# Attention mask products in float32r instead of bfloat16, in a hybrid decoder trunk

## The chip, the cores and the metric

One NeuronCore of a Trainium2 chip runs the whole program in one launch. The metric is device time in microseconds (us), lower is better. Engines are named as in the profile: PE is TensorE's matrix product, PEld its weight load, DVE is VectorE, ACT is ScalarE, POOL is GpSimd, SP is SyncE, which here only issues DMAs.

## The reference

Two layers, 512 tokens of width 1024 in float32. Each layer is SwiGLU (width 2816), a mixer, SwiGLU, with a residual and a layer norm behind each. The mixer joins two kinds of softmax-like attention with a gated delta rule and projects the result:

```
def diff_attention_block(q_blk, start, k1, k2, v, lam):
    causal = s[None, :] <= t[:, None]
    def probs(qi, ki):
        sc = einsum('bhqd,bhkd->bhqk', qi, ki) * A_QK_DIM ** -0.5
        return softmax(where(causal, sc, -inf), axis=-1)
    w = probs(q1, k1) - lam * probs(q2, k2)
    return einsum('bhqk,bhkd->bhqd', w, v)            # 4 heads, 2 x 32 wide, values 64

def stick_breaking_block(q_blk, start, k, v):         # 4 heads of 64
    strict = s[None, :] < t[:, None]
    z = einsum('bhqd,bhkd->bhqk', q_blk, k) * B_HEAD_DIM ** -0.5
    log_stay = where(strict, log_sigmoid(-z), 0.0)
    log_tail = cumsum(log_stay, axis=3, reverse=True) - log_stay
    w = where(strict, exp(log_sigmoid(z) + log_tail), 0.0)
    return einsum('bhqk,bhkd->bhqd', w, v)

# the delta rule solves, in chunks, (I + strict_lower(k_beta k^T * decay)) [u, w] = rhs
# and then scans over the chunks with a state per head
```

## The kernel before

Activations stand feature-major, 128 features by 512 tokens in a tile. Every float32 matrix is split into a high and a low part in float32r, and a product of two is three PE products (`mm3`, lines 103 to 105): high x high, high x low, low x high. Weights come in chunks of 512 KB by DMA (`wraw`, line 81, mostly issued by SP), are cast by ACT (line 89, `whi`) and subtracted by DVE or POOL (line 90, `wlo`).

In the mixer, a layer's attention runs in units: a block of 128 queries (`qt`) of one head against the `n = (qt + 1) * 128` keys up to it. `scores` (line 872) makes a unit's scores in a PSUM bank: one or two products of float32r operands (line 880, one for the diff attention, two for the stick-breaking one), and then the mask product of line 881, which adds the mask to the 128 columns on the diagonal, as identity times mask. The mask is 0 or `NEG`; for it two bfloat16 constants, `identb` and `maskb`, were made at the start. Behind the mask come the row maximum on DVE (line 917), the exponential on ACT (line 467, in the helper `act`), the difference of the two softmaxes on DVE (lines 922 to 926), transposes on PE (line 904), a copy on ACT (906) and the product with the values (line 909). A unit's transposes are recorded behind the next unit's scores (`later`).

`attend(which, j)` goes through eight units of two heads. The stick-breaking attention (`which` 1) comes first in a mixer, then the projections of the delta rule, then `triangles()`: for each of four heads, products (line 594), the decays (lines 663 to 665), the matrix `LT` (line 673), its way to a scratch in DRAM (line 675), and then `base`, which reads the diagonal blocks of 16 x 16 (line 692, tile `blk`), inverts them on DVE in thirty small steps (lines 700 and 702), writes them back (lines 703 and 705) and reads the whole matrices `XT` and `X` (lines 708 and 710, the latter in a tile named `inv`). `attend(0, 0)`, the first two heads of the diff attention, is written behind `triangles()`, and in its middle the second projection of its queries and keys, whose weight products (lines 103 to 105) and stacking copies (`stack`: DVE cast of line 511, small DMAs of line 524 on SP) fill in. `delta()` doubles and joins the inverse (lines 718, 723, 738, 745); `outputs()` is the scan.

The order on each engine is not the order of the text: a scheduler takes each engine's next instruction from those that are ready by its own estimate, so an instruction more or less in one place can lay the order out anew behind it. Each engine's queue, SP's included, is then strictly in order.

The constants are loaded by POOL's DMAs in `constants()`, recorded behind the first SwiGLU's gate products. Two of the three scratch tensors are filled with zeros there, by DMAs from a small tile `zero` of the constants' pool that POOL clears at the program's start. Tiles named `lt` come from a pool of five buffers that the layer norms, the SwiGLU and the mixers share.

Of the kernel before, what the change touches and what calls it, by code (L numbers as in the profile page):

```python
# [9 lines left out]
F32 = mybir.dt.float32  # L10
F32R = mybir.dt.float32r
BF16 = mybir.dt.bfloat16
# [4 lines left out]
P = 128  # L17
# [353 lines left out]
        run((), g.pending)  # L371


NEG = -1.0e30
HEADS = 4
NC = T // P
SB = 16
# [3 lines left out]
def const_masks():  # L381
    r = np.arange(P)
    row, col = r[:, None], r[None, :]
    ms = [
        np.where(col >= row, 0.0, NEG),
        (row <= col).astype(np.float64),
    ]
    ms.append(((row // (2 * SB) == col // (2 * SB)) & (row // SB % 2 == 0) & (col // SB % 2 == 1)).astype(np.float64))
    ms.append(np.where(col <= row, 0.0, NEG))
    ms.append(np.where(col < row, 0.0, NEG))  # L390
    return np.stack(ms, axis=1).astype(np.float32)
# [31 lines left out]
def ch(c):  # L423
    return slice(c * P, (c + 1) * P)


def mixer(g, l):
    nc = g.nc
# [16 lines left out]
    def py():  # L445
        return psc.tile([P, T], F32, name="psc")
# [103 lines left out]
    n = 2 * HEADS  # L550
# [323 lines left out]
    def scores(q, k, qt, i, which):  # L874

        n = (qt + 1) * P
        dgn = ch(qt)
        sc = py()
        for j, t in enumerate(k[i]):
            nc.tensor.matmul(out=sc[:, 0:n], lhsT=q[i][0][:, dgn], rhs=t[:, 0:n], start=j == 0, stop=False)  # L880
        nc.tensor.matmul(out=sc[:, dgn], lhsT=g.identb, rhs=g.maskb[:, which], start=False, stop=True)
        return sc

    def attend(which, j, between=None):
# [13 lines left out]
    def unit(which, qt, h, po, su, col):  # L898
# [13 lines left out]
        def diff():  # L912
            mx = sm.tile([P, 2], F32, name="mx")
            pr = []
            for i in range(2):
                sc = scores(qa, ka, qt, 2 * h + i, 0)
                nc.vector.tensor_reduce(out=mx[:, i:i + 1], in_=sc[:, 0:n], axis=mybir.AxisListType.X, op=ALU.max, negate=True)
                p = at.tile([P, T], F32, name="at")
                act(out=p[:, 0:n], in_=sc[:, 0:n], func=AF.Exp, bias=mx[:, i:i + 1], accum_out=su[:, i:i + 1])
                pr.append(p)  # L920
            cf = sm.tile([P, 2], F32, name="cf")
            nc.vector.reciprocal(out=cf[:, 0:1], in_=su[:, 1:2])
            nc.vector.scalar_tensor_tensor(out=cf[:, 1:2], in0=su[:, 0:1], scalar=g.nlam[:, l:l + 1], in1=cf[:, 0:1],
                                           op0=ALU.mult, op1=ALU.mult)
            p1, p2 = pr
            nc.vector.scalar_tensor_tensor(out=p1[:, 0:n], in0=p2[:, 0:n], scalar=cf[:, 1:2], in1=p1[:, 0:n],
                                           op0=ALU.mult, op1=ALU.add)
            return lambda: values(p1)
# [150 lines left out]
def program(ctx, tc, a, out, mixer=None):  # L1079
    g = Ctx()  # L1080
    g.tc = tc
    g.nc = nc = tc.nc
    g.out = out
    g.a = a
    cp = ctx.enter_context(tc.tile_pool(name="const", bufs=1))
    g.cp = cp
    g.dp = ctx.enter_context(tc.tile_pool(name="scratch", bufs=1, space=bass.MemoryType.DRAM))
    g.wr = ctx.enter_context(tc.tile_pool(name="wr", bufs=2))
    g.ws = ctx.enter_context(tc.tile_pool(name="ws", bufs=WS))
    g.xp = ctx.enter_context(tc.tile_pool(name="xp", bufs=24))  # L1090
    g.lnp = ctx.enter_context(tc.tile_pool(name="lnp", bufs=5))
    g.sm = ctx.enter_context(tc.tile_pool(name="sm", bufs=2))
    g.ps = ctx.enter_context(tc.tile_pool(name="ps", bufs=2, space=bass.MemoryType.PSUM, reuse_waits="tile"))
    g.st = Stream(g, a["w"])

    g.ones = cp.tile([P, P], F32, name="ones")
    nc.gpsimd.memset(g.ones, 1.0)
    g.ident = cp.tile([P, P], F32, name="ident")
    nc.gpsimd.affine_select(out=g.ident, in_=g.ones, pattern=[[-1, P]], compare_op=ALU.is_equal, fill=0.0,
                            base=0, channel_multiplier=1)  # L1100

    def after(later, first, sync=False):
        kind = mybir.DependencyClass.Sync if sync else mybir.DependencyClass.NoSync
        tc.add_manual_dep(later.ins, first.ins.name, mybir.DependencyInfo(kind, mybir.DependencyReason.DATA), reason="order")

    g.after = after
    nln = DEPTH * 3 * KD
    g.lng = cp.tile([P, nln], F32, name="lng")
    g.lnb = cp.tile([P, nln], F32, name="lnb")
    small = ("conv", "dtb", "alog", "dng", "dfg", "sbg")  # L1110
    for nm in small:
        setattr(g, nm, cp.tile(list(a[nm].shape), F32, name=nm))
    g.mask = cp.tile([P, NMASK - 2, P], F32, name="mask")
    g.maskb = cp.tile([P, 2, P], BF16, name="maskb")
    g.identb = cp.tile([P, P], BF16, name="identb")
    nc.vector.tensor_copy(out=g.identb, in_=g.ident)
    g.ba = cp.tile([P, DEPTH, KD, 4 * HEADS], F32R, name="ba")
    g.nlam = cp.tile([P, DEPTH], F32, name="nlam")
    n = HEADS * NC * SLAB // P
    zero = cp.tile([P, n // 16], F32, name="zero")  # L1120
    nc.gpsimd.memset(zero, 0.0)
    g.scr = [g.dp.tile([P, n], F32, name=f"scr{i}") for i in range(3)]

    def constants():

        def load(out, in_):
            g.after(nc.gpsimd.dma_start(out=out, in_=in_), g.mark, True)

        raw = g.lnp.tile(list(a["ba"].shape), F32, name="lt")
        load(raw, a["ba"])  # L1130
        part = g.ba[:, :, :, 0:2 * HEADS]
        nc.scalar.copy(out=part, in_=raw)
        nc.vector.tensor_tensor(out=g.ba[:, :, :, 2 * HEADS:], in0=raw, in1=part.bitcast(F32), op=ALU.subtract)
        load(g.lng, a["lng"])
        load(g.lnb, a["lnb"])
        load(g.mask, a["mask"][:, 0:NMASK - 2])
        for nm in small:
            load(getattr(g, nm), a[nm])
        lb = g.lnp.tile([P, DEPTH, 4, 32], F32, name="lt")
        load(lb, a["lamb"])  # L1140
        mb = g.lnp.tile([P, 2, P], F32, name="lt")
        load(mb, a["mask"][:, NMASK - 2:NMASK])
        nc.vector.tensor_copy(out=g.maskb, in_=mb)
        for l in range(DEPTH):
            init = 0.8 - 0.6 * math.exp(-0.3 * l)
            nc.vector.tensor_scalar(out=g.dfg[:, l:l + 1], in0=g.dfg[:, l:l + 1], scalar1=1.0 - init, scalar2=None, op0=ALU.mult)
            dv = lb[:, l].rearrange("p (a b) d -> p a b d", b=2)
            nc.vector.tensor_tensor(out=dv[:, :, 0], in0=dv[:, :, 0], in1=dv[:, :, 1], op=ALU.mult)
            le = g.sm.tile([P, 2], F32, name="lam")
            nc.vector.tensor_reduce(out=le, in_=dv[:, :, 0], axis=mybir.AxisListType.X, op=ALU.add)  # L1150
            nc.scalar.activation(out=le, in_=le, func=AF.Exp)
            lv = g.nlam[:, l:l + 1]
            nc.vector.tensor_tensor(out=lv, in0=le[:, 1:2], in1=le[:, 0:1], op=ALU.subtract)
            nc.vector.tensor_scalar(out=lv, in0=lv, scalar1=-init, scalar2=None, op0=ALU.add)
        for t in g.scr[1:]:
            load(t.rearrange("p (a b) -> p a b", a=16), zero.unsqueeze(1).to_broadcast([P, 16, n // 16]))

    g.constants = constants
    g.wctx = ExitStack()

    def more_weights():
        g.wx = g.wctx.enter_context(tc.tile_pool(name="wx", bufs=WX, side="right", reuse_waits="tile"))

    g.more_weights = more_weights
    more_weights()
    g.x = []
    g.st.use([g.ws])
    with tc.tile_pool(name="x0", bufs=KD) as x0:
        for k in range(KD):
            if k % 4 == 0:  # L1170
                for b in range(2):
                    g.st.get(2 * k + b * PC)
            t = x0.tile([P, T], F32, name="x0")
            nc.sync.dma_start(out=t, in_=a["xT"][k * P:(k + 1) * P])
            hi = g.xp.tile([P, T], F32R, name="x")
            lo = g.xp.tile([P, T], F32R, name="x")
            nc.scalar.copy(out=hi, in_=t)  # L1177
            nc.vector.tensor_tensor(out=lo, in0=t, in1=hi.bitcast(F32), op=ALU.subtract)
            g.x.append((hi, lo))
    g.pending = ()  # L1180
    for l in range(DEPTH):
        ffn(g, 3 * l, False, True)
        if mixer:
            mixer(g, l)
        ffn(g, 3 * l + 2, l == DEPTH - 1, False)
    g.wctx.close()
# [72 lines left out]
```

## Time and profile before

| | |
|---|---|
| time, median of 3 runs | 2249.18 us (2244.98 to 2249.8) |
| the profiled execution | 2250.16 us, span 2248.4 us |
| PE busy | 2138.2 us, 95% of the span |
| PE's weight load busy | 1782.6 us, 79% |
| DVE, ACT, POOL busy | 1169.6, 907.9, 377.5 us |
| granted clock of TensorE | 0.985 of full speed, mean of the span |

Busy times of PE are unions of intervals that overlap: a product's row lasts until its last result is written, while the next has begun. The share of the span therefore says little on how much faster a product could come behind the one before it; the distance from one start to the next does. Where the clock is granted at 0.5, TensorE runs at 1.2 GHz, else at 2.4 GHz; a share between them is a mean over the stretch.

### The profile page before, as it was taken

To read this page: it belongs to the slowest core of one execution; us is meant where nothing else is said; L and a number is where in the kernel's file an instruction comes from. 1 tells how busy PE (TensorE), PEld (TensorE's weight loads), DVE (VectorE), ACT (ScalarE), POOL (GpSimd) and SP (SyncE) were. 2 spreads that over 40 slices of the span, in tenths; PEclk is the share of its full clock that TensorE was granted. 3 is DMA by queue.
4 is the path that set the end of the run, shared out by engine and by line. 5 is a ranking of instruction groups with operands and counts; after the bars stand their busy time and mean duration, and the time that the engine had idled before them with its cause. 6 is when DMAs were issued, how large, how long until landed. Compare 5 with 4: busy or idle time off the path is not lost. (4 is left out here: it accounts for less than half of the span.)

```text
span 2248.4 us, 30132 instructions
## 1 busy us (share of the span) xinstructions
PE 2138.2 (95%) x11382; PEld 1782.6 (79%) x11382; DVE 1169.6 (52%) x2363; ACT 907.9 (40%) x1801; POOL 377.5 (17%) x327
## 2 busy tenths in 40 slices
PE   8999999999798999999999999999987989999997
PEld 7888889777677888888888888897776768888886
DVE  4533436386578833343663334263774788333426
ACT  4333324575464533332443333245753535333313
POOL 1100011426204400000130000023461234000010
PEclk9999999999899999999999999999998999999998
DMA  6423323514512233332333333234144123333322
GB/s 190 125 94 95 98 75 104 139 40 122 129 58 72 84 109 94 94 94 75 116 109 95 94 94 94 66 104 131 57 133 109 48 85 94 95 96 100 95 66 94
DMA packets 90898, 217.32 MB, mean 97 GB/s; under 512 B 21968, under 2 KB 36336, under 8 KB 90752
## 3 DMA queue, kind: packets, MB, share of 16 engines
q1 hardware_dynamic: 82848, 187.47, 27.5%
q10 hardware_dynamic: 6912, 25.17, 3.8%
q0 software_dynamic: 992, 2.75, 0.7%
q8 instruction: 90, 1.47, 0.3%
q14 instruction: 56, 0.46, 0.1%
HBM read 193.83 MB, written 6.83 MB: 89 GB/s over the span
## 5 line engine op out<-in xcount | busy, mean ns | idle before, releaser
L89 ACT CAST whi<-wraw 128x512 fp32r<-128x512 f32 x692 | 421.4, 619 | 959.4 <-PE pd L104 755.1
L90 DVE TENSOR_TENSOR wlo<-wraw,whi 128x512 fp32r<-128x512 f32 x580 | 431.0, 751 | 658.6 <-ACT whi L89 647.4
L103 PE MATMUL pd<-x,whi 128*128 128x512 f32 (+1 forms) x1920 | 726.7, 380 | 12.9 <-ACT x L1177 6.2
L105 PE MATMUL pd<-x,wlo 128*128 128x512 f32 (+1 forms) x1920 | 728.3, 380 | 3.2 <-DVE wlo L90 3.2
L104 PE MATMUL pd<-x,whi 128*128 128x512 f32 (+1 forms) x1920 | 727.7, 379 | 1.6 <-POOL x L231 1.3
L103 PEld LDWEIGHTS pd<-x,whi 128*128 128x128 f32 x1920 | 365.8, 191 | 77.5 <-ACT x L1177 6.2
L105 PEld LDWEIGHTS pd<-x,wlo 128*128 128x128 f32 x1920 | 366.2, 191 | 67.4 <-DVE wlo L90 3.4
L104 PEld LDWEIGHTS pd<-x,whi 128*128 128x128 f32 x1920 | 366.2, 191 | 66.8 <-POOL x L231 3.0
L103 PE MATMUL pd<-hhi,whi 128*128 128x512 f32 (+1 forms) x880 | 307.7, 350 | 0.0
L104 PE MATMUL pd<-hlo,whi 128*128 128x512 f32 (+1 forms) x880 | 307.7, 350 | 0.0
L105 PE MATMUL pd<-hhi,wlo 128*128 128x512 f32 (+1 forms) x880 | 307.3, 349 | 0.0
L168 POOL TENSOR_TENSOR lt<-lt 128x512 f32<-128x512 f32 x26 | 38.9, 1497 | 1065.3 <-ACT lt L165 1065.3
L103 PEld LDWEIGHTS pd<-hhi,whi 128*128 128x128 f32 x880 | 165.5, 188 | 24.4
L105 PEld LDWEIGHTS pd<-hhi,wlo 128*128 128x128 f32 x880 | 165.4, 188 | 24.1
L104 PEld LDWEIGHTS pd<-hlo,whi 128*128 128x128 f32 x880 | 165.5, 188 | 24.1
L90 POOL TENSOR_TENSOR wlo<-wraw,whi 128x512 fp32r<-128x512 f32 x112 | 150.2, 1357 | 138.7 <-ACT whi L89 70.1
L259 DVE TENSOR_TENSOR lt<-pd,lt 128x512 f32<-128x512 f32 x88 | 60.4, 689 | 111.9 <-PE pd L105 110.7
L231 POOL TENSOR_TENSOR x<-x 128x256 fp32r<-128x256 f32 x60 | 45.1, 753 | 162.5 <-ACT x L229 132.7
L134 POOL TENSOR_TENSOR x<-x 128x512 f32<-128x512 f32 x48 | 70.9, 1522 | 0.0
L261 DVE TENSOR_TENSOR hlo<-lt,hhi 128x512 fp32r<-128x512 f32 x88 | 67.0, 765 | 6.3
L165 ACT ACTIVATE lt<-x 128x256 f32<-128x256 f32 (+1 forms) x58 | 29.7, 512 | 95.8 <-DVE x L163 95.5
L568 DVE SCALAR_TENSOR_TENSOR kqv<-pd,conv,kqv 128x511 f32<-128x511 f32 (+2 forms) x72 | 53.5, 743 | 20.1 <-ACT kqv L566 18.9
(309 smaller groups left out, 2287.9 us busy)
## 6 DMA issues: line engine op xcount, KB each, us to landing
wraw<-in_w SPq DMA_DIRECT2D x308, 512.0 KB, 3.5
wraw<-in_w ACTq DMA_DIRECT2D x48, 512.0 KB, 3.6
kqv<-kqv SPq DMA_DIRECT2D x128, 64.0 KB, 2.0
kqv<-kqv SPq DMA_DIRECT2D x48, 128.0 KB, 4.7
scr<-zero POOLq DMA_DIRECT2D x2, 1032.0 KB, 11.1
x<-in_xT SPq DMA_DIRECT2D x8, 256.0 KB, 5.5
scr<-inv SPq DMA_DIRECT2D x8, 256.0 KB, 2.7
XT<-scr SPq DMA_DIRECT2D x8, 256.0 KB, 4.8
```

The source lines that it names most:

```text
L89: nc.scalar.copy(out=hi, in_=r)
L90: (eng or self.eng or nc.vector).tensor_tensor(out=lo, in0=r, in1=hi.bitcast(F32), op=ALU.subtract)
L103: nc.tensor.matmul(out=out, lhsT=whi, rhs=xhi, start=first, stop=False)
L104: nc.tensor.matmul(out=out, lhsT=whi, rhs=xlo, start=False, stop=False)
L105: nc.tensor.matmul(out=out, lhsT=wlo, rhs=xhi, start=False, stop=last)
L134: i = g.nc.gpsimd.tensor_tensor(out=t, in0=xhi.bitcast(F32), in1=xlo.bitcast(F32), op=ALU.add)
L165: nc.scalar.activation(out=sq[:, r], in_=t[:, r], func=AF.Square)
L168: eng.tensor_tensor(out=self.acc2[:, r], in0=self.acc2[:, r], in1=sq[:, r], op=ALU.add)
L231: eng.tensor_tensor(out=xlo[:, r], in0=t[:, r], in1=xhi[:, r].bitcast(F32), op=ALU.subtract)
L259: nc.vector.tensor_tensor(out=sg, in0=pu, in1=sg, op=ALU.mult)
L261: nc.vector.tensor_tensor(out=hlo, in0=sg, in1=hhi.bitcast(F32), op=ALU.subtract)
L568: nc.vector.scalar_tensor_tensor(out=y[:, s:], in0=p[:, :T - s], scalar=wc[:, 3 - s:4 - s], in1=y[:, s:], op0=ALU.mult, op1=ALU.add)
```

## The change

The identity and the mask of the mask products become float32r tiles (`identr`, `maskr`), as the scores' operands are; `NEG` becomes a power of two. Where a bfloat16 product has a weight-load instruction of its own in the program, a float32r product loads its weights itself, so 96 load instructions leave the program (48 mask products in each layer). The constants' pool gives up the tile `zero`; the zeros come from an `lt` buffer instead, cleared and sent to the scratch behind the other loads of `constants()`.

```
-NEG = -1.0e30
+NEG = -2.0 ** 100
...
-        nc.tensor.matmul(out=sc[:, dgn], lhsT=g.identb, rhs=g.maskb[:, which], start=False, stop=True)
+        nc.tensor.matmul(out=sc[:, dgn], lhsT=g.identr, rhs=g.maskr[:, which], start=False, stop=True)
...
-    g.maskb = cp.tile([P, 2, P], BF16, name="maskb")
-    g.identb = cp.tile([P, P], BF16, name="identb")
-    nc.vector.tensor_copy(out=g.identb, in_=g.ident)
+    g.maskr = cp.tile([P, 2, P], F32R, name="maskr")
+    g.identr = cp.tile([P, P], F32R, name="identr")
+    nc.vector.tensor_copy(out=g.identr, in_=g.ident)
...
-    zero = cp.tile([P, n // 16], F32, name="zero")
-    nc.gpsimd.memset(zero, 0.0)
...
-        nc.vector.tensor_copy(out=g.maskb, in_=mb)
+        nc.vector.tensor_copy(out=g.maskr, in_=mb)
...
+        zero = g.lnp.tile([P, n // 16], F32, name="lt")
+        nc.gpsimd.memset(zero, 0.0)
         for t in g.scr[1:]:
             load(t.rearrange("p (a b) -> p a b", a=16), zero.unsqueeze(1).to_broadcast([P, 16, n // 16]))
```

The order changes with it. On PE, in the first layer's `attend(0, 0)`, the units with 512 keys stand in a row before (`psc` is the scores' bank, `pd` a bank of weight products, `pt` one of transposes):

```order
L880 MATMUL psc<-kqv 128x512
L881 LDWEIGHTS identb
L881 MATMUL psc<-maskb,identb 128x128
L880 MATMUL psc<-kqv 128x512
L881 LDWEIGHTS identb
L881 MATMUL psc<-maskb,identb 128x128
L904 MATMUL pt<-ident,at 128x128 x3
L880 MATMUL psc<-kqv 128x512
```

In the new program the same place of PE's order reads:

```order
L880 MATMUL psc<-kqv 128x512
L881 MATMUL psc<-maskr,identr 128x128
L104 MATMUL pd<-x,whi 128x512
L105 MATMUL pd<-x,wlo 128x512
L103 MATMUL pd<-x,whi 128x512
L104 MATMUL pd<-x,whi 128x512
L105 MATMUL pd<-x,wlo 128x512
L103 MATMUL pd<-x,whi 128x512
L104 MATMUL pd<-x,whi 128x512
L105 MATMUL pd<-x,wlo 128x512
L904 MATMUL pt<-ident,at 128x128 x3
```

Eight weight products have moved between the first score of 512 columns and the transposes. A little later on PE, in the units with 256 keys of the same two heads, the order of before has weight products between the attention's (`po` is the bank of the output):

```order
L880 MATMUL psc<-kqv 128x256
L881 LDWEIGHTS identb
L881 MATMUL psc<-maskb,identb 128x128
L103 MATMUL pd<-x,whi 128x512
L104 MATMUL pd<-x,whi 128x512
L909 MATMUL po<-kqv,at 128x64 x4
L904 MATMUL pt<-ident,at 128x128 x4
L105 MATMUL pd<-x,wlo 128x512
L880 MATMUL psc<-kqv 128x128
```

and now the units with 256 and 128 keys follow each other:

```order
L880 MATMUL psc<-kqv 128x256
L881 MATMUL psc<-maskr,identr 128x128
L909 MATMUL po<-kqv,at 128x64 x4
L904 MATMUL pt<-ident,at 128x128 x4
L880 MATMUL psc<-kqv 128x128
```

The weight products are gone from there. On SP, around the inverse of the first layer, the four scratch writes, the weight load, the read of the blocks and the small copies of the stacked queries and keys stand so before:

```order
L675 DMA scr_98<-inv 128x4x128 x4
L81 DMA wraw<-in_w 128x1024
L692 DMA blk<-scr_98 128x16x16
L524 DMA kqv<-kqv 32x512 x12
L703 DMA scr_99<-blk 128x16x16
```

and so in the new program (the scratch tensors' numbers have moved by two):

```order
L675 DMA scr_96<-inv 128x4x128 x3
L524 DMA kqv<-kqv 32x512 x2
L675 DMA scr_96<-inv 128x4x128
L524 DMA kqv<-kqv 32x512 x2
L81 DMA wraw<-in_w 128x1024
L692 DMA blk<-scr_96 128x16x16
L81 DMA wraw<-in_w 128x1024
L524 DMA kqv<-kqv 32x512 x7
L703 DMA scr_97<-blk 128x16x16
```

Four of the small copies now stand ahead of the read of the blocks, two of them ahead of the last scratch write.

## Rows read from the trace of the kernel before

**Rows 1.** The page, part 1: engine, busy us (share), instructions.

```profile
PE 2138.2 (95%) x11382; PEld 1782.6 (79%) x11382; DVE 1169.6 (52%) x2363; ACT 907.9 (40%) x1801; POOL 377.5 (17%) x327
```

**Rows 2.** Line 881 alone (duration ns min/median/max); then costliest groups (busy us, mean ns).

```profile
L881 PEld LDWEIGHTS <-identb x96: 94/96/153, 432.6 to 1772.2; 128*128 128x128 bf16 x96
L881 PE MATMUL psc<-maskb,identb x96: 219/230/330, 432.6 to 1772.3; 128*128 128x128 bf16 x96
...
L103 PEld LDWEIGHTS pd<-x,whi 128*128 128x128 f32 x1920 | 365.8, 191 | 77.5 <-ACT x L1177 6.2
```

**Rows 3.** Windows: stretch us, length, busy us (instructions) by engine, granted clock, DMA share, GB/s.

```profile
565.00:581.00 16.00, 12.20 (x52) 8.80 (x50) 13.18 (x36) 9.54 (x27) 9.32 (x9) 0.69 0.55 132
581.00:595.00 14.00, 11.11 (x77) 9.30 (x76) 12.41 (x54) 7.14 (x23) 2.55 (x2) 0.99 0.17 40
...
1680.00:1695.00 15.00, 10.85 (x47) 7.89 (x46) 12.60 (x34) 8.66 (x25) 8.42 (x9) 0.77 0.57 140
```

**Rows 4.** Timeline of PE, 568 to 603 us: start, us, ..., [idle before <-releaser].

```profile
569.90 0.45 PE L880 MATMUL psc<-kqv 128*128 128x384 f32 x1 [1.54 <-ACT at L467]
...
572.31 0.80 PE L880 MATMUL psc<-kqv 128*128 128x512 f32 x1 [1.27 <-ACT at L467]
...
601.92 2.04 PE L718 MATMUL pa<-inv,lt 128*128 128x128 f32 x8 [3.36 <-DMA inv<-scr]
```

**Rows 5.** Timeline of PE, around a mask before weight products.

```profile
446.20 0.39 PE L105 MATMUL pd<-x,wlo 128*128 128x512 f32 x1
446.43 0.40 PE L880 MATMUL psc<-kqv 128*128 128x256 f32 x2
446.68 0.23 PE L881 MATMUL psc<-maskb,identb 128*128 128x128 bf16 x1
446.71 0.47 PE L103 MATMUL pd<-x,whi 128*128 128x512 f32 x1
447.03 0.40 PE L104 MATMUL pd<-x,whi 128*128 128x512 f32 x1
```

**Rows 6.** Timeline of PE, a mask before transposes.

```profile
439.51 0.23 PE L881 MATMUL psc<-maskb,identb 128*128 128x128 bf16 x1
439.58 0.50 PE L904 MATMUL pt<-ident,at 128*128 128x128 f32 x3
```

**Rows 7.** Timeline of PE, other products of 128 columns.

```profile
545.81 1.06 PE L594 MATMUL po<-kqv 128*128 128x128 f32 x8
546.71 1.06 PE L594 MATMUL pt<-kqv 128*128 128x128 f32 x8
...
585.71 0.22 PE L880 MATMUL psc<-kqv 128*128 128x128 f32 x1
585.78 0.23 PE L881 MATMUL psc<-maskb,identb 128*128 128x128 bf16 x1
```

**Rows 8.** Timeline of POOL, 40 to 300 us.

```profile
40.57 1.18 POOL L1127 DMA_DIRECT2D scr<-zero  x1
53.26 1.13 POOL L1127 DMA_DIRECT2D scr<-zero  x1 [11.51 <-issue]
...
234.43 0.54 POOL L1127 DMA_DIRECT2D lt<-in_mask  x1 [10.33 <-DVE hlo L261]
287.02 1.55 POOL L168 TENSOR_TENSOR lt<-lt 128x512 f32<-128x512 f32 x1 [52.05 <-ACT lt L165]
```

**Rows 9.** Timeline of DVE, 577 to 594 us.

```profile
577.66 0.16 DVE L700 TENSOR_TENSOR blkt<-blk 128x15 f32<-128x15 f32 x1
...
580.96 0.42 DVE L917 TENSOR_REDUCE mx<-psc 128x1 f32<-128x256 f32 x1 [2.39 <-PE psc L881]
...
586.04 0.29 DVE L917 TENSOR_REDUCE mx<-psc 128x1 f32<-128x128 f32 x1 [0.64 <-PE psc L881]
...
593.86 0.37 DVE L704 COPY blk<-blk 128x256 f32<-128x256 f32 x1
```

## The prediction

> **What bounds the kernel now.** I read the summary first, then the line of the changed product, then the stretch in which TensorE loses time. TensorE (PE) is busy 2138.2 of 2248.4 us, VectorE (DVE) 1169.6 us [rows 1]; so a change pays by what it takes off PE's stream, or off the moments in which PE stands still or runs slowly. The mask product is one of 96 PE instructions with a mean near 230 ns, and its own weight load takes 96 ns, against 191 ns for a load of float32r weights [rows 2]. These durations overlap from one instruction to the next, so I price everything by the distance from one start to the next.
>
> PE's losses lie thick in one place, in each of the two layers: the first two heads of the diff attention, beside the triangular inverse. From 565 to 581 us PE is busy 12.20 of 16 us at a granted clock of 0.69 (of 1.0, so 1.2 GHz for 10 of the 16 us and 2.4 GHz for the rest), and the second layer has the same at 1680 to 1695 us (0.77) [rows 3]. There PE waits 1.54 and 1.27 us for the exponentials on ScalarE (ACT), and later 3.36 us for the inverse to come back from memory [rows 4].
>
> **Price of the products themselves, before.** A 512-column weight product takes 0.23 us from start to start (446.20 to 446.43). Mask product plus the weight product behind it take 0.35 us (446.68 to 447.03). So the bf16 mask costs 0.12 us, although its row is followed 0.03 us later by the next start: the product behind it pays [rows 5]. In front of a transpose it costs 0.07 us (439.51 to 439.58) [rows 6]. In the program's order of before, 62 of the 96 masks stand before a weight or score product and 34 before something else: 62 x 0.12 + 34 x 0.07 = 9.8 us.
>
> **After.** The trace has no 128-column mask in float32r. Its nearest kin is the 128-column score product, float32r too: 0.07 us to the next start (585.71 to 585.78), but with the short bf16 load behind it, so this is the low end. With full-length loads behind them, 128-column products run at 0.11 us (eight in 0.90 us, 545.81 to 546.71). The high end is that a narrow float32r product takes as long as a 512-column one, 0.23 us [rows 5, 7]. I take 0.11 us, because in the new kernel the load behind is always a full-length one: 96 x 0.11 = 10.6 us, so **+0.8 us**, with ends at 96 x 0.07 = 6.7 us (-3.1 us) and 96 x 0.23 = 22.1 us (+12.3 us). The separate weight-load instruction of the mask goes, but the load stays.
>
> The loads in the rows differ by a factor of two, 96 against 191 ns [rows 2]. If the 95 ns more were open at each mask, 96 x 95 ns = 9.1 us would be added; it is the third rival below. What I hold against it is [rows 5]: behind the short load and its product, the next product is 0.09 us late (0.32 us to its successor instead of 0.23), so the short load's advantage is not seen in the distances. The Trainium skill has the rule that speaks against the change: by "TensorE: Matmul & The Clock Gate", section "Weight-path perf modes", a fast load reads weights 32 bits at a time, two of bf16, with no win for fp32. The factor of two in the trace agrees with it; by that rule alone the sum would be those 9.1 us higher.
>
> **What else is removed or moved.** The zeros of the scratch: their memset and two DMAs leave the place before the residual sums and stand behind the load of the mask on GpSimd (POOL). POOL issued them at about 41 and 53 us, waiting 11.51 us between the two; now it can do so from about 235 us, and is free near 250 us. The next thing that POOL does is at 287.02 us [rows 8], so some 37 us cover it: price nothing. The zeros now hold one of the five `lt` buffers until the second DMA lands, but the statistics that need that buffer back belong to the same 287 us. If the cover were gone, the stall would be of the size of that wait, 11.5 us. The early stretch gains nothing, since nothing in front of PE waited for POOL there. The casts of identity and mask on DVE stay one for one. NEG is a value.
>
> **The new order.** With 96 load instructions fewer and other operands, the scheduler lays PE's order out anew in both mixers. I counted weight products (rows of lines 103 to 105) between attention products in the first diff attention beside the inverse. From the first 512-column score to the first 256-column score: 5 before, 18 after (and 4 more just ahead). From there to the last transpose: 19 before, 2 after. Between that and the wait for the inverse: 8 before, 6 after. So PE's filling moves to where it stood still, and leaves the stretch behind. What this is worth goes by DVE, which makes the inverse (577.66 to 593.86 us, thirty small steps among the softmax) and is busy 12.41 of 14 us there [rows 3, 9]. In that time DVE itself waited for PE's scores 2.39 and 0.64 us [rows 9], while PE was at the lower clock and had weight products between the scores. Those two waits, 3.0 us, are what can go per layer; I take half, since the softmax steps in front of the inverse come a step earlier in DVE's queue and a cast stands before the last triangle: **-1.5 us per layer, -3.0 us in both**. The low end is nothing at all. The high end is both waits in full and the waits of PE for ACT (2.8 us) once, 5.8 us per layer.
>
> Against that, SyncE (SP) gets four small copies of the stacked heads around the last scratch write, and a weight load before the read of the blocks stays. SP's order is strict, so a copy that waits for DVE's cast holds the inverse back. I price that under the rivals.
>
> **The sum.** +0.8 - 3.0 = -2.2 us on the profiled execution's 2250.16 us (span 2248.4 us): 2248.0 us. The median shown, 2249.18 us, lies 1.0 us below the profiled time, so the forecast on the median is about **2247 us**.
>
> **Rivals.**
> 1. *The new order gives much more.* PE stays at 2.4 GHz through the 512-column units and DVE's waits go in full: 2 x 5.8 = 11.6 us less, +0.8: about 2238 us. For it: 10 us at 1.2 GHz per layer in [rows 3]. Against it: the filling is taken from the next stretch, where DVE, not PE, sets the pace, and the slow clock may simply come there.
> 2. *The inverse starts later (slower).* SP's four copies wait for DVE's cast of the keys, and the last scratch write and the read of the blocks wait behind them; PE has only 6 weight products (1.4 us) to cover what comes on top of its 3.36 us wait for the inverse [rows 4]. Each copy held up for a us is a us at the end. With 2 to 3 us of delay per layer and 0.5 us less cover (two products), 5 to 7 us: about 2255 us. It decides as soon as the delay passes DVE's saving of 1.5 us.
> 3. *The mask product is dear in float32r*, by its load (+9.1 us) or because a narrow product is as slow as a wide one (+12.3 us), with the order's -3.0 us: 2255 to 2258 us. Against it: the 0.07 us of the narrow score.
> 4. *Nothing happens*: the order's parts cancel and 0.11 is 0.10: 2249 us.
>
> **How the numbers follow.** Forecast (2244 to 2250 us) 0.45, rival 1 0.20, rival 2 0.16, rival 3 0.08, rival 4 0.11. A measurement of this kernel tells about 0.2%, 4.5 us, from no change: 2244.7 to 2253.7 us counts as the same. Of the forecast 0.32 lies inside and 0.13 below; of rival 2, 0.02 inside. Faster 0.20 + 0.13 = 0.33; same 0.32 + 0.11 + 0.02 = 0.45; slower 0.14 + 0.08 = 0.22. The range goes from 2237 us (rival 1 but for its end) to 2258 us (rivals 2 and 3 but for the dearest).
>
> **What would show it.** Right: from a mask product in float32r to the next start some 0.11 us, and the product behind it no longer late, 0.23 us to its successor. In the inverse's first stretch PE's waits for ACT under 1 us and the clock near 1.0, with a lower clock or new waits in the 256- and 128-column units behind; the inverse's last step no later than in before. Wrong: 0.2 us from mask to next start in float32r (rival 3); scratch writes or the read of the blocks that stand behind the small copies on SP, and a wait for the inverse well above 3.4 us (rival 2); POOL's first sum of squares after 287 us (the zeros).

## The result: 0.7% slower, and the profile after

The changed kernel takes 2264.55 us (median of 6 runs, 2258.5 to 2269.06) against 2249.46 us (2244.98 to 2251.1) of the kernel before on the same chip: ratio 1.0069, 95% interval [1.0055, 1.0084]. On another chip it came to 1.0074 [1.0059, 1.009]. The forecast was 2247 us; the time lies above the range, and above every rival in it. The profiled execution has a span of 2266.9 us at a mean granted clock of 0.979, where before had 2248.4 us and 0.985.

The first part of the page of the changed kernel, and the line of the mask products alone (weight load, product), answer [rows 1] and the first lines of [rows 2]:

```profile
PE 2148.1 (95%) x11382; PEld 1801.9 (79%) x11382; DVE 1176.8 (52%) x2363; ACT 910.0 (40%) x1801; POOL 378.8 (17%) x327
```

```profile
L881 PEld LDWEIGHTS psc<-maskr,identr x96: 186/189/333, 440.3 to 1782.9; 128*128 128x128 f32 x96
L881 PE MATMUL psc<-maskr,identr x96: 218/223/415, 440.4 to 1782.9; 128*128 128x128 f32 x96
```

PE is busy 9.9 us more and idle 8.6 us more. The load of a mask's weights doubled (96 to 189 ns), the product itself is as long as it was.

**The stretch the forecast looked at.** The windows around the first two heads of the diff attention answer [rows 3], and PE's two longest waits there answer [rows 4]:

```profile
574.00:590.00 16.00, 13.41 (x71) 10.16 (x69) 15.41 (x37) 9.02 (x26) 10.74 (x10) 0.99 0.58 146
590.00:604.00 14.00, 13.07 (x58) 11.82 (x57) 11.11 (x55) 7.62 (x25) 1.27 (x1) 0.50 0.27 72
```

```profile
587.85 0.50 PE L880 MATMUL psc<-kqv 128*128 128x512 f32 x1 [1.83 <-ACT at L467]
...
611.11 2.05 PE L718 MATMUL pa<-inv,lt 128*128 128x128 f32 x8 [4.04 <-DMA inv<-scr]
```

The first window went from a clock of 0.69 to 0.99 and PE from 12.20 to 13.41 us busy; the low clock came in the next window instead (0.99 to 0.50), and the wait for the inverse grew from 3.36 to 4.04 us (in the second layer it fell, from 4.80 to 4.18 us). From the first product of line 594 to the last of line 758, the inverse and what lies around it, the layers took 105.7 and 106.6 us before and take 103.0 and 101.3 us now (starts of those products). Three weight products, 0.7 us, have left this stretch (137 before, 134 now); the rest of the 2.7 and 5.3 us is a gain. The first product on the finished inverse (line 718) comes 1.2 and 1.4 us sooner behind the first of line 594, near the 1.5 us that were forecast.

**What is paid back ahead of it.** From a layer's first score (line 880) to the first product of line 594, the stick-breaking attention and the projections, it is 116.3 and 115.7 us before and 119.2 and 119.0 us after, with 336 weight products in each. It is so in every trace with the new order: 117.8 to 121.0 us, against 114.2 to 117.6 us in every trace with the old one. So about 3 us per layer are lost there, most of what the inverse gains; no run shows why.

**Where it is lost: the scan behind it.** From that last product of line 758 to the last small step of the scan's outputs (DVE, line 818) it is 46.6 and 46.5 us before, and 55.1 and 54.4 us after: some 8 us per layer. POOL first, the casts of the attention outputs (L995) and the residual sums (L134), before and after:

```profile
674.32 4.16 POOL L995 TENSOR_TENSOR kqv<-x,kqv 128x256 fp32r<-128x256 f32 x6 [6.93 <-ACT kqv L994]
678.43 10.38 POOL L134 TENSOR_TENSOR x<-x 128x512 f32<-128x512 f32 x8
```

```profile
682.36 4.51 POOL L995 TENSOR_TENSOR kqv<-x,kqv 128x256 fp32r<-128x256 f32 x6 [6.49 <-ACT kqv L994]
686.82 10.31 POOL L134 TENSOR_TENSOR x<-x 128x512 f32<-128x512 f32 x8
```

Now DVE in those moments, the square root of the first outputs' scale with one scan step (L792, L775) between; before, and then after:

```profile
674.09 0.15 DVE L114 TENSOR_TENSOR orr_t<-of 128x4 f32<-128x4 f32 x1
674.27 0.16 DVE L115 SCALAR_TENSOR_TENSOR orr_t<-orr_t,oms 128x4 f32<-128x4 f32 x1
674.47 0.59 DVE L116 SCALAR_TENSOR_TENSOR of<-orr_t,of 128x4 f32<-128x4 f32 x1
...
677.16 0.65 DVE L818 TENSOR_TENSOR of<-of,sqs 128x4 f32<-128x4 f32 x1
677.84 1.19 DVE L819 TENSOR_TENSOR o<-o,of 128x512 f32<-128x512 f32 x1
678.96 0.59 DVE L775 SCALAR_TENSOR_TENSOR inv<-pa,neG,inv 128x128 f32<-128x128 f32 x2
```

```profile
683.39 0.41 DVE L781 TENSOR_TENSOR vn<-pa,brk 128x256 f32<-128x256 f32 x1
...
684.18 0.66 DVE L116 SCALAR_TENSOR_TENSOR of<-orr_t,of 128x4 f32<-128x4 f32 x1
...
686.82 0.33 DVE L792 SCALAR_TENSOR_TENSOR S<-S,eG,pa 128x128 f32<-128x128 f32 x1
687.08 1.04 DVE L114 TENSOR_TENSOR orr_t<-of 128x4 f32<-128x4 f32 x1
688.04 0.33 DVE L792 SCALAR_TENSOR_TENSOR S<-S,eG,pa 128x128 f32<-128x128 f32 x1
688.29 1.04 DVE L115 SCALAR_TENSOR_TENSOR orr_t<-orr_t,oms 128x4 f32<-128x4 f32 x1
689.37 1.20 DVE L116 SCALAR_TENSOR_TENSOR of<-orr_t,of 128x4 f32<-128x4 f32 x1
690.60 1.19 DVE L818 TENSOR_TENSOR of<-of,sqs 128x4 f32<-128x4 f32 x1
691.83 1.71 DVE L819 TENSOR_TENSOR o<-o,of 128x512 f32<-128x512 f32 x1
693.47 0.59 DVE L775 SCALAR_TENSOR_TENSOR inv<-pa,neG,inv 128x128 f32<-128x128 f32 x2
```

A step of four columns takes 0.15 us alone, mostly 0.65 us beside POOL's casts of 256 columns and 1.04 to 1.20 us beside its sums of 512, near the 1.3 us that one of the eight sums takes on average. Steps that read PSUM (line 792 from `pa`, line 781) keep their 0.33 and 0.41 us. Before, the last small step ended as the sums began; after, four of them and the scaling of the outputs (line 819) fall beside the sums, and the scan step of line 775 stands behind them in DVE's queue. PE waits for it and falls to the lower clock; the wait, and the window from 690 us:

```profile
693.95 1.20 PE L779 MATMUL pa<-inv,XT 128*128 128x128 f32 x4 [2.55 <-DVE inv L775]
```

```profile
690.00:700.00 10.00, 7.45 (x32) 6.17 (x32) 5.03 (x8) 0.98 (x4) 7.13 (x6) 0.55 0.00 0
```

Over the 52 small steps of a layer's outputs, the time above 0.165 us each adds up to 2.6 us before and 6.6 us after. These 4.0 us, 0.5 us for the scaling and 0.7 us for the three weight products that now stand in the scan's stretch (58 before, 61 after) make some 5 of the 8 us. The rest is not taken apart; part of it is the lower clock (0.907 and 0.969 over the two scans, 1.00 before). The Trainium skill has a rule for the slow steps in "SBUF — State Buffer", section "Who interferes with whom": a DVE instruction with two inputs in SBUF contends with a GpSimd instruction that reads SBUF, and their shared port pair is an exclusive lock. The rows agree, and the steps that are spared have one of their inputs in PSUM.

**The zeros.** POOL's rows answer [rows 8]; behind them ACT's waits for weights and PE's:

```profile
246.96 0.21 POOL L1154 MEMSET lt<- 128x129 f32 x1 [10.36 <-DVE hlo L261]
247.50 1.14 POOL L1125 DMA_DIRECT2D scr<-lt  x1 [0.33 <-POOL lt L1154]
260.22 1.13 POOL L1125 DMA_DIRECT2D scr<-lt  x1 [11.57 <-issue]
294.92 1.55 POOL L168 TENSOR_TENSOR lt<-lt 128x512 f32<-128x512 f32 x1 [33.57 <-ACT lt L165]
```

```profile
273.04 1.14 ACT L89 CAST whi<-wraw 128x512 fp32r<-128x512 f32 x2 [8.26 <-DMA wraw<-in_w]
```

```profile
276.43 0.77 PE L155 MATMUL pa<-lt,ones 128*128 128x512 f32 x1 [3.66 <-ACT lt L154]
```

POOL had the room it was thought to have. But the transfers go where the weights of the first down projection come just in time; the windows of before, then after (DMA share is the last but one column):

```profile
260.00:273.00 13.00, 12.97 (x56) 10.15 (x56) 4.76 (x8) 3.84 (x7) 0.00 (x0) 1.00 0.34 111
273.00:285.00 12.00, 12.00 (x53) 9.67 (x52) 7.21 (x13) 3.12 (x5) 0.00 (x0) 1.00 0.30 87
```

```profile
260.00:273.00 13.00, 12.78 (x56) 10.08 (x54) 3.19 (x5) 2.61 (x5) 1.13 (x1) 1.00 0.87 154
273.00:285.00 12.00, 8.57 (x25) 6.80 (x26) 7.92 (x13) 4.27 (x8) 0.00 (x0) 0.72 0.25 77
```

PE loses 3.4 us of busy time in the last window and runs part of it at the lower clock. The k-th weight product is 1.7 us late at 260 us and 7.9 us late at 280 us. I took that for 6 of the 15 us.

### The profile page after: what moved, and what is told of

Read it like the earlier page. It is cut to its first block, busy times and chain, and to the rows that moved or that the text cites. A ratio compares the mean times of both kernels' runs of the same rounds, so it can differ in the third digit from the quotient of the medians.

```text
span 2266.9 us, 30145 instructions
## 1 busy us (share of the span) xinstructions
PE 2148.1 (95%) x11382; PEld 1801.9 (79%) x11382; DVE 1176.8 (52%) x2363; ACT 910.0 (40%) x1801; POOL 378.8 (17%) x327
## 5 line engine op out<-in xcount | busy, mean ns | idle before, releaser
L90 POOL TENSOR_TENSOR wlo<-wraw,whi 128x512 fp32r<-128x512 f32 x112 | 150.6, 1355 | 153.0 <-ACT whi L89 106.6
L134 POOL TENSOR_TENSOR x<-x 128x512 f32<-128x512 f32 x48 | 71.2, 1525 | 0.0
## 6 DMA issues: line engine op xcount, KB each, us to landing
scr<-lt POOLq DMA_DIRECT2D x2, 1032.0 KB, 12.2
```

The source lines that it names most:

```text
L90: (eng or self.eng or nc.vector).tensor_tensor(out=lo, in0=r, in1=hi.bitcast(F32), op=ALU.subtract)
L134: i = g.nc.gpsimd.tensor_tensor(out=t, in0=xhi.bitcast(F32), in1=xlo.bitcast(F32), op=ALU.add)
```

## The experiments

All are whole kernels, timed in five rounds against the kernel before on the same chip. An order was held by chaining each engine's instructions as they stand in the kernel named, for the scheduler alone, without a wait on the chip:

```diff
+ for a, b in zip(at, at[1:]):   # places of one engine's instructions, in the wanted order
+     tc.add_manual_dep(eng[e][b], eng[e][a].name, DependencyInfo(DependencyClass.NoSync, ...))
```

**Zeros early, new order.**

```diff
+ zero = cp.tile([P, n // 24], F32, name="zero"); nc.gpsimd.memset(zero, 0.0)   # program's start
- zero = g.lnp.tile([P, n // 16], F32, name="lt"); nc.gpsimd.memset(zero, 0.0)  # in constants()
```

> The changed kernel, but its zeros are set and sent at the program's start, as in the kernel before (from a constant tile of a 24th of the scratch). The order of PE is the changed kernel's to the last instruction. Theory (the slowdown of 15.1 us has two parts: the zeros' transfers take the bandwidth of the weights of the first down projection, 6.2 us in the traces; the new order loses the rest in the scan): 2264.6 - 6.2 = about 2258 us, 1.004 of before, and the windows at 247 to 273 us show the DMA share near 0.3 again. Rival (the zeros are innocent, the order alone has it): 2264 us. Rival (the zeros have it all): 2250 us.

1.0072 [1.0059, 1.0085], 2263.55 us. The stall at 270 us is gone from the trace, the time is not. My theory of two causes fell here. Once more, on another chip:

> The run with early zeros once more (1.0072 of before in its first measurement), to stand on the same chip as the run with the zeros sent twice. If the zeros cost 6 us under the new order too, this comes out at 1.004 to 1.005.

1.0064 [1.0049, 1.0079].

**Zeros late, old order** (the kernel before with the zeros' lines of the change).

> The kernel before (masks in bfloat16, its own order of PE to the last instruction), but its zeros are moved as in the change, behind the load of the mask. Theory: +6.2 us, about 2255.5 us, 1.0028 of before; ACT waits for the weight chunks near 260 and 273 us and PE drops to the lower clock there. Rival (a chance of those runs): 2249.5 us, the same as before. The prediction's own figure for this move was nothing, or 11.5 us if its cover were gone.

1.0031 [1.0021, 1.0042], 2253.56 us: here the theory held.

**Float32r masks in the old order, bfloat16 masks in the new one**, zeros early in both.

> Masks in float32r, zeros early, and every engine's order held to that of the kernel before, instruction by instruction. What is left of the change is the price of 96 products alone. Theory (the product costs what the prediction said, 0.11 us each to the next start against 0.12 with what followed): +1 us or less, 2249 to 2250.5 us. Rival (the masks are dear in float32r, by their full weight load, 96 x 95 ns, and the order is innocent): 2258 us.

1.0017 [1.0007, 1.0026].

> The kernel before (masks in bfloat16, zeros early), with every engine's order held to that which the float32r masks gave. Theory (the order loses some 8 us in the scans of the two layers, whatever the masks are made of): 2257 to 2259 us. Rival (the masks are dear and the order is innocent): 2249.5 us. If order and product act apart, this run and the one with the old order add up to the run with early zeros.

1.0056 [1.0043, 1.0069], 2259.0 us. So the order has most of it whatever the masks are made of, and the two act apart: 1.0017 times 1.0056 is 1.0073, and both together were 1.0072 and 1.0064. In the run with the old order PE's rows stand as in [rows 5], with the other mask:

```profile
447.40 0.22 PE L881 MATMUL psc<-maskr,identr 128*128 128x128 f32 x1
447.46 0.44 PE L103 MATMUL pd<-x,whi 128*128 128x512 f32 x1
447.74 0.39 PE L104 MATMUL pd<-x,whi 128*128 128x512 f32 x1
```

Mask and the product behind it take 0.34 us; it was 0.35. In front of transposes the mask is dearer, 0.14 instead of 0.07 us to the next start (median of the 14 such places where PE does not wait; 0.11 us in the changed kernel). Over all 96, from the product ahead of the mask to the second start behind it, the sum is 1.7 us more than in the trace of before.

**Sums held to the scan's end.** The orders of PE, DVE, ACT and SP are the kernel's own; POOL waits.

```diff
-        nm.residual(d)
+        nm.residual(d, g.scanend, True)   # waits for the last step of line 818
```

> The changed kernel itself, once more, so that it stands on the same chip as the three runs beside it. By its first measurement 1.0069 of before.

1.0074 [1.0059, 1.009].

> The changed kernel with the orders of PE, DVE, ACT and SP held to its own, and one edit: POOL's eight residual sums in each mixer wait until DVE has done the last small step of the scan's outputs. In the changed kernel POOL's casts and sums run from 682.36 to 697.13 us, and DVE's small steps beside them take 0.65 to 1.20 us instead of 0.16: some 12 of them on the path to the scan's next product, about 6 us more than alone, in each layer. Theory (this is where the new order loses): the sums leave that path, 4 to 5 us less per layer (the casts stay), of which DVE's wide steps at the start of the out projection may give back 1 to 2: about 2257 to 2259 us, 1.004 of before, and small steps at 0.16 to 0.2 us behind the casts. Rival (the scan is late by PE's order alone, the small steps are only onlookers): 2264 us. Rival (the sums, now late, hold up the out projection): over 2266 us.

1.0096 [1.0079, 1.0112]: the second rival, and slower than the changed kernel. Yet the scan itself came out as the theory had it: 48.0 us in both layers instead of 54 to 55, small steps 2.8 us above their own time instead of 6.6. All of that and more went back behind the scan, where DVE's wide steps now stand beside the sums; DVE of the kernel before, then of this one, and PE of this one:

```profile
698.89 1.29 DVE L1025 TENSOR_TENSOR x<-x,kqv 128x512 f32<-128x512 f32 x2 [1.51 <-ACT x L827]
700.10 1.43 DVE L995 TENSOR_TENSOR kqv<-x,kqv 128x256 fp32r<-128x256 f32 x4
```

```profile
701.73 3.10 DVE L1025 TENSOR_TENSOR x<-x,kqv 128x512 f32<-128x512 f32 x2 [1.51 <-ACT x L827]
704.75 5.71 DVE L995 TENSOR_TENSOR kqv<-x,kqv 128x256 fp32r<-128x256 f32 x4
```

```profile
707.69 0.80 PE L104 MATMUL pd<-kqv,whi 128*128 128x512 f32 x1 [3.03 <-DVE kqv L995]
```

From the last step of line 818 to the first product of line 155, a statistic of the layer norm, it is 16.2 us instead of 8.0. The six wide steps take 8.8 us instead of 2.7, so the collision only moved; I had allowed 1 to 2 us for it.

> The kernel before with the orders of PE, DVE, ACT and SP held to its own, and the same edit: POOL's residual sums wait for the last small step of the scan's outputs. There only some 7 small steps stood beside POOL, about 2 us more than alone. Theory: 1.5 us less per layer at the scan, as much given back at most at the out projection: 2245 to 2249 us. If the gain here is as large as in the run with the new order, the steps beside POOL do not explain the difference of the two orders.

1.0062 [1.0047, 1.0078], 2262.08 us: not the theory's 2245 to 2249 us, but the kernel before, made slower by putting its sums beside the wide steps. Its scan gained 0.5 us per layer, and behind it 7.7 and 8.2 us were lost.

> The changed kernel with both repairs: the zeros early, as in the first run, and the residual sums held as beside. Theory (both causes act, and apart from each other): 6 us under the run with the sums held alone, about 2251 to 2253 us. Rival (the zeros' 6 us at 270 us are won back elsewhere under the new order, as the timed runs with early zeros say: 1.0072 against 1.0069): the same as the run with the sums held alone.

1.009 [1.0073, 1.0106]: the rival; early zeros help 0.06% here, less than the intervals tell apart.

**Sums held to the first outputs only.**

```diff
-        nm.residual(d)
+        nm.residual(d, g.half, True)      # line 818 of the second pair's first outputs
```

> The changed kernel with the orders of PE, DVE, ACT and SP held to its own, and POOL's residual sums held back only to the last small step of the scan's first outputs (of its second chunk), which in the kernel before had come just ahead of them by itself. The sums then run while DVE waits for PE in the third and fourth chunk, and are done before the out projection, whose wide steps they slowed in the run that held them to the end. Theory (the new order loses because these small steps now fall beside the sums): four steps at 1.04 to 1.20 us become 0.2 us and the scaling behind them 0.7 us in place of 1.71, some 4.5 us less per layer with nothing given back: 9 us under the changed kernel, about 2256 us, 1.003 to 1.004 of before. Rival (the loss moves to the steps of the last outputs): 2262 us or more.

2254.22 us, 1.0026 [1.0015, 1.0037], 10 us under the changed kernel, as the theory had it. POOL and DVE of this run (one line was added, so the scaling is line 820):

```profile
684.09 10.38 POOL L134 TENSOR_TENSOR x<-x 128x512 f32<-128x512 f32 x8 [1.22 <-DVE of L818]
```

```profile
683.07 0.15 DVE L114 TENSOR_TENSOR orr_t<-of 128x4 f32<-128x4 f32 x1
683.14 0.33 DVE L792 SCALAR_TENSOR_TENSOR S<-S,eG,pa 128x128 f32<-128x128 f32 x1
683.40 0.15 DVE L115 SCALAR_TENSOR_TENSOR orr_t<-orr_t,oms 128x4 f32<-128x4 f32 x1
683.59 0.16 DVE L116 SCALAR_TENSOR_TENSOR of<-orr_t,of 128x4 f32<-128x4 f32 x1
683.78 0.17 DVE L818 TENSOR_TENSOR of<-of,sqs 128x4 f32<-128x4 f32 x1
683.98 0.69 DVE L820 TENSOR_TENSOR o<-o,of 128x512 f32<-128x512 f32 x1
```

The same four steps take 0.15 to 0.17 us, the scaling 0.69 instead of 1.71. The scans take 48.5 us, PE no longer waits for line 775 there, and the clock from 690 to 700 us is 1.00 instead of 0.55, and over both scans 1.00. The hold costs POOL a wait of 1.22 us.

> The kernel before with bfloat16 masks and its own early zeros, the order that the float32r masks gave, and the sums held to the same step as in the run beside. It was 2259.0 us (1.0056) without the hold. Theory: 9 us less, 2249 to 2250 us, the same as before, so that the new order with that repair costs no more than the old one and keeps what it gained at the inverse. Rival (the order loses elsewhere too): 2254 us or more.

2250.25 us, 1.0003 [0.9992, 1.0014]. With bfloat16 masks, the new order with this one wait is as fast as the old order: what the order lost in the time goes with the collision. The theory's other half, that it keeps what it gained at the inverse, does not show: against the trace of before, the stretch ahead takes 1.5 and 3.7 us more, the inverse's stretch 2.6 and 6.0 us less, the scan 1.9 and 2.0 us more. These parts cancel. The same wait in the old order was not timed; there the sums begin 0.6 us behind that step by themselves. No version tried is faster than the kernel before.

**The zeros, dosed.**

> The changed kernel, but the zeros are sent twice, one pair of transfers behind the other, at the same place (order of PE as it is). With the run of early zeros beside it and the changed kernel between them this doses the zeros: none, once, twice beside the weights of the first down projection. Theory (each pair holds those weights back, 5 to 6 us in the traces): 10 to 12 us over the run with early zeros. Rival (what is lost there is won back later, as the timed runs under the new order say): less than 3 us over it.

1.0068 [1.0052, 1.0085]: two pairs of transfers cost no more than one or none under the new order.

> The kernel before (bfloat16 masks, its own order) with the zeros moved as in the change and sent twice. One pair cost 1.0031 there. Theory (each pair costs its stall of 4 to 6 us under the old order): 1.0055 to 1.006. Rival (the stall is won back or only the first pair stalls, and 1.0031 was partly scatter): 1.001 to 1.003, the same as with one pair, as under the new order, where none, one and two pairs gave 1.0064 to 1.0072, 1.0069 to 1.0074 and 1.0068.

1.0011 [1.0001, 1.0022]: the rival; two pairs cost less than the 1.0031 of one.

> Masks in bfloat16, every engine held to the changed kernel's order, zeros late as in the change. The same with early zeros was 1.0056. Theory (the zeros' cost goes with the place, 0.3%, whatever the order): 1.0087. Rival (under the new order the zeros cost next to nothing in the total): 1.0055 to 1.006.

1.0064 [1.0042, 1.0085], against 1.0056 with early zeros: the interval is too wide to part theory and rival by itself.

> Masks in float32r, every engine held to the order of the kernel before (with late zeros), zeros late as in the change. The same with early zeros was 1.0017. Theory (the zeros cost 0.3% under the old order): 1.0048. Rival (less than 0.1%): 1.0017 to 1.0027. With these two every combination of mask, order and zeros has been timed.

1.0012 [1.0001, 1.0023], against 1.0017 with early zeros: the rival.

Late less early zeros is thus +0.31% (bfloat16, old order), -0.05% (float32r, old), +0.08% (bfloat16, new) and +0.04% (float32r, new, means of two measurements each), each of them good to 0.10 to 0.25%. The stall itself is real: PE stands still 2.4 to 3.8 us between 255 and 300 us in all nine traces with late zeros, and 0.03 us in the eight with early ones. In the pair with float32r masks and the old order, the k-th weight product is 4.2 us late at 280 us (0.7 us of that already at 260 us), 2.8 us at 480 us and 0.3 us at 640 us: there it is made up in the mixer. In the other pairs 3.3 to 7.9 us of lateness are still there at 640 us, and two traces of the changed kernel alone differ by 4.3 us there. So where the stall is won back, and why the first pair alone kept a loss, stays open.

## Why the prediction was wrong, point by point

- **"The new order: -1.5 us per layer, -3.0 us in both" is the step that failed**, in sign and size: the order measured alone cost 0.56%, some 12.6 us. Its mechanism was right for the place it looked at: the finished inverse reaches PE 1.2 and 1.4 us sooner, and the stretch around it gained 2.7 and 5.3 us. (One reading was off: at DVE's second wait, 0.64 us at 586 us, PE was no longer at the lower clock, 0.99 from 581 us on [rows 3].) But the term ended where the counting of weight products ended. The order also moves what stands ahead, about 3 us per layer more, and what comes behind, the scan, 8 us per layer more. The scan was not looked at: the POOL rows of the sums and the DVE steps of the scan's outputs were in the trace of before, with the lengthening beside POOL (0.50 to 0.66 us a small step, 1.19 us the scaling) already to be seen. That the order's loss in the time hangs on this collision is shown by the hold of POOL's sums, which takes 10 to 12 us off and leaves PE's and DVE's orders as they are. Even without the collision the -3.0 us did not come: 1.0003 [0.9992, 1.0014] is -1.8 to +3.1 us.
- **Rivals 1 and 2** looked in the same place. PE's clock did rise in the first units, and fell in the next, as rival 1 had weighed. The read of the blocks came no later, 28.5 instead of 28.6 us behind the first product of line 594, so the copies on SP of rival 2 held nothing back; PE's wait for the inverse grew by 0.7 us in one layer and fell by 0.6 us in the other. The slower side was foreseen with the wrong mechanism.
- **The masks, "+0.8 us" (-3.1 to +12.3).** Right in mechanism: 0.11 us from mask to next start in front of transposes in the changed kernel, next to nothing lost in front of weight products, and of the 9.1 us for the doubled load little shows. By the traces it is 1.7 us, timed 0.17%, 3.8 us (1.6 to 5.8), within the bounds; rival 3 (9 to 12 us) is excluded.
- **The zeros, "price nothing".** The reason given was wrong: what was to be covered was not POOL's time but the weights' transfers, and the sign named for it (POOL's first sum of squares after 287 us) came, at 294.92 us. In the total it was nearly right, but not for its reason: three of four pairs within 0.1%.
- **The sum as measured**: 0.17% and 0.56% make 0.73%, with nothing for the zeros; the change is 0.69 to 0.74%.

## What to carry to other kernels

When a change lets a scheduler lay an order out anew, compare the order from the stage's start to its end, not only where the change's gain is expected: what one stretch gains, the ones beside it may pay back. And look for short serial steps of DVE with both inputs in SBUF: what POOL does beside them sets their time. Such POOL work wants a place tied to the steps, not the one where its inputs happen to come free; and moving it wholesale behind them may set it beside the next ones. An idle issuing engine does not make a transfer free: ask whose data are just in time while it runs.

## What the runs showed of the hardware

A DVE step of 0.15 us with both inputs in SBUF cost 0.65 to 1.20 us beside POOL, one of 0.69 us up to 1.71 us, while POOL's eight sums took 10.3 us beside DVE's small steps, 10.4 us with hardly any of them beside, and 12.2 us beside its wide ones. A weight load of float32r that is twice as long as that of bfloat16 (189 against 96 ns) moved the starts of the products around it by 1.7 us in all 96 places together.
